# Who writes the identity halves of the scan's stacks at the border between two phases

## The chip, the core and the metric

The kernel runs on one core of a Trainium2 chip. Its engines are TensorE (PE in the profile, its weight loads PEld), VectorE (DVE), ScalarE (ACT), GpSimd (POOL) and SyncE (SP), which here only issues DMAs. The metric is device time in microseconds (us); a lower number is better.

## The reference

One inference step of one layer, for 128 context tokens and 2048 latent tokens of width 1024, in float32:

```python
def _layer(x, mod, s0, is_latent, lp):
    shift, scale, gate = jnp.split(mod, 3, axis=-1)
    h = _rmsnorm(x, lp['norm_g']) * (1.0 + scale) + shift
    proj = h @ lp['w_in']                                   # 1024 -> 4096
    r, k, v, g_a, b_gate, c_gate, u_conv, g_b = jnp.split(proj, IN_SPLITS, axis=-1)
    ...                                                     # token shift of r, k, v
    ya, s_final = _wkv(h, r, k, v, s0, lp)                  # 8 heads x 64, two directions
    ya = ya.astype(x.dtype) * jax.nn.silu(g_a)
    yb = b_gate * _short_conv(c_gate * u_conv, lp['conv_w'], is_latent) * jax.nn.silu(g_b)
    u = jnp.concatenate([ya, yb], axis=-1) @ lp['w_out']
    return x + gate * u, s_final

    # inside _wkv: the scan over tokens, for each direction and head
    def step(S, inp):
        r_t, w_t, k_t, v_t, kk_t, a_t = inp
        s_kk = jnp.einsum('bdhij,bdhj->bdhi', S, kk_t)
        S = (S * w_t[..., None, :] - s_kk[..., :, None] * (kk_t * a_t)[..., None, :]
             + v_t[..., :, None] * k_t[..., None, :])
        return S, jnp.einsum('bdhij,bdhj->bdhi', S, r_t)
```

The outputs are the normalised new context and latent tokens and the final context states of the scan.

## The kernel before

The kernel has three phases. **Phase 1** projects the tokens in six blocks with float32 products split into three matmuls (lines 182 to 184), makes the scan's operands from them and stores these in DRAM (`scr_ops`, `scr_vt` and others); its last part is the gated convolution (`groupB`, lines 546 to 621), which stores its result `ov` to `mixT` in line 621. **Phase 2** is the scan, cut into chunks of 64 tokens and 17 stages; a stage handles eight chunks of one direction (gi 0) and eight of the other (gi 1). **Phase 3** is the output projection.

A stage of phase 2 goes as follows. The operands `rr` are loaded (line 1009). Products of them are taken on TensorE (`Gm`, `Fm`, line 1019, and the transposes `Qm`, line 1028) and written out of PSUM, masked, by VectorE and ScalarE into one of three slots with the tiles `F`, `GA` and `Q` (lines 1037, 1048 and 1051). VectorE folds and transposes blocks of `GA` into `ab` (lines 1058, 1063, 1081, 1082). GpSimd inverts 32x32 triangles by substitution: 45 instructions on `ztmp` and `zt` (lines 1091 and 1094), a chain within itself. VectorE transposes the result twice (`zr`, line 1102, `zd`, line 1105), and the halves are merged into the tile `zb` by ScalarE copies and TensorE products: `zb` from `zd` (line 1111), the product `U` (line 1119) and its copy into `zd` (line 1122), the product `W` (line 1127) and its copy into `zb` (line 1130). The product `X` of `F` and `zb` (line 1171) is copied, negated, into a stack by ScalarE (line 1175). Two stacks together give the operators `E` (line 1189 and, masked, 1194), which the sequential part `S` (lines 1220 and 1246) applies chunk by chunk.

A stack is a tile of 128 partitions with two halves of columns, `b` = 0 and 1. Its bottom partitions are written new in each stage, by ScalarE (lines 1160, 1161, 1175); the top partitions of half 1 are loaded by DMA (line 956); the top partitions of half 0 hold identities and are filled once, in `presetS`. There are six stacks: `stf` (two) for line 1175 and `stg` and `sth` (two each) for lines 1160 and 1161, in even and in odd stages.

The pools decide where memory comes from. Phase 2 begins inside phase 1 with its first two stages (`early`), and at the end of phase 1 `setup_rest` opens the pools that take the memory that phase 1 gives back. There the stacks are made and filled, `zb` is cleared by GpSimd (line 907), and a third slot of `F`, `GA`, `Q` (numbers 20 and 21) is made, whose `GA21` lies over memory of phase 1's last `ov`: the first write of `GA21` waits until the store of `ov` has landed.

The engines take their instructions in order. In phase 1's recurrence and from stage 0 of the main loop on the order is written out by hand; at the border of the two phases a scheduler places instructions by its own estimate of their times.

Of the kernel before, what the change touches and what calls it, by code (L numbers as in the profile page):

```python
# [815 lines left out]
def phase2(K):  # L816
    nc, tc, A, S = K.nc, K.tc, K.A, K.S
    V, G, P, T = nc.vector, nc.gpsimd, nc.scalar, nc.tensor
    D = nc.sync.dma_start
    MF, MG, ME = (0, 1), (0, 1), (2, 3)  # L820
    B = Ctx()
# [39 lines left out]
    def setup_rest():  # L861
        O.l0 = Pool(K, "p2l0", "left")
        O.l1 = Pool(K, "p2l1", "left")
        O.pS = Pool(K, "p2S", "left", 4, PSUM)
        O.p2 = Pool(K, "p2s", "left", 2, PSUM)
        O.r2 = Pool(K, "p2r2", "right")
        new_slot(O.r2)
        cp = O.l0
        vec = cp.tile([128, 4], F32, name="vec2")
        D(vec[:], A["vec"][:, V_GW:V_GW + 4])  # L870
        B.gwh = cp.tile([128, 4], F32, name="gwh")
        V.tensor_scalar(B.gwh[:], vec[:], 0.5, None, ALU.mult)
        B.geps = cp.tile([128, 1], F32, name="geps")
        V.memset(B.geps[:], 64e-5)
        B.pc = cp.tile([64, 2, 8, 34], F32, name="pc")
        for d in range(2):
            D(B.pc[:, d], S[f"pc{d}"].rearrange("(e c) n -> c e n", c=64))

        B.fs = ring(O.l1, 2, [128, 2, 2, 8, 64], "stf", presetS)
        B.gs = ring(O.l1, 2, [128, 2, 2, 8, 64], "stg", presetS)  # L880
        B.gs2 = ring(O.r2, 2, [128, 2, 2, 8, 64], "sth", presetS)
        B.zb = O.l1.tile([128, 16, 64], F32, name="zb")
        zero(B.zb)
# [29 lines left out]

    def presetS(t_):
        for hd in range(2):
            V.tensor_copy(t_[0:64, 0, hd], B.I2[0:64].unsqueeze(1).broadcast_to((64, 8, 64)))

    def tl(shape, tag, b, pool=None, dt=F32):
        return (pool or O.l0).tile(shape, dt, tag=tag, name=f"{tag}_{K.u()}", bufs=b)
# [729 lines left out]
```

## Time and profile before

| | |
|---|---|
| median of 3 runs | 1607.61 us (1599.0 to 1609.05) |
| the profiled execution | 1596.26 us |
| its span, first to last instruction | 1594.5 us |
| PE busy | 1502.0 us (94%) |
| DVE busy | 1137.4 us (71%) |
| ACT busy | 772.3 us (48%) |
| POOL busy | 574.6 us (36%) |
| the border: from GpSimd's clearing of `zb` to its inversion of stage 3 | 948.49 to 988.83 us |

Starts and lengths are in us from the span's start. A row of a timeline has start, length, engine, line, operation, output and inputs, and the count; in square brackets stands the idle time of the engine before it and who ended it. Consecutive instructions of one engine overlap a little at their ends, so the distance from one start to the next is the time that an instruction holds its engine. A row of a table by stretches has, after the stretch, its length, the busy time and count of PE, PEld, DVE, ACT and POOL, then the granted TensorE clock, the DMA share and GB/s.

### The profile page before, as it was taken

To read this page: it belongs to the slowest core of one execution; us is meant where nothing else is said; L and a number is where in the kernel's file an instruction comes from. 1 tells how busy PE (TensorE), PEld (TensorE's weight loads), DVE (VectorE), ACT (ScalarE), POOL (GpSimd) and SP (SyncE) were. 2 spreads that over 40 slices of the span, in tenths; PEclk is the share of its full clock that TensorE was granted. 3 is DMA by queue.
4 is the path that set the end of the run, shared out by engine and by line. 5 is a ranking of instruction groups with operands and counts; after the bars stand their busy time and mean duration, and the time that the engine had idled before them with its cause. 6 is when DMAs were issued, how large, how long until landed. Compare 5 with 4: busy or idle time off the path is not lost.

```text
span 1594.5 us, 39396 instructions
## 1 busy us (share of the span) xinstructions
PE 1502.0 (94%) x16208; PEld 1382.7 (87%) x16208; DVE 1137.4 (71%) x1960; ACT 772.3 (48%) x1460; POOL 574.6 (36%) x961
## 2 busy tenths in 40 slices
PE   5899999999999999999999989999999997699998
PEld 2799999999999998999999987887888886478786
DVE  5889996673999645449984447898998986546533
ACT  4456662432555213136541127878787787323221
POOL 0033331001333100013223606888888876112221
PEclk7799999999999999999999999999999998899999
DMA  9659999663788865438886536566667655445442
GB/s 372 206 153 268 268 266 337 209 223 116 227 221 215 234 222 181 145 114 243 257 247 241 204 120 187 158 169 198 168 189 199 159 150 166 128 141 181 146 148 93
DMA packets 204580, 313.79 MB, mean 197 GB/s; under 512 B 58088, under 2 KB 147560, under 8 KB 190320
## 3 DMA queue, kind: packets, MB, share of 16 engines
q1 hardware_dynamic: 168816, 311.13, 63.1%
q10 hardware_dynamic: 35584, 0.14, 1.5%
q8 instruction: 127, 2.08, 0.6%
q14 instruction: 53, 0.43, 0.1%
HBM read 208.05 MB, written 103.17 MB: 195 GB/s over the span
## 4 chain that ended last, share of the span: by engine, by line
PE 62%; DVE 14%; POOL 9%; DMA 6%; issue 5%; ACT 2%; SPq 1%; ACTq 0%; DVEq 0%; POOLq 0%
POOL zt L1094 6%; PE psE L1189 4%; PE psu L1503 4%; PE psu L1505 4%; PE psu L1504 4%; POOL ztmp L1091 3%; PE mmb L182 2%; PE mmb L184 2%; PE mmb L183 2%; PE mmc L182 2%; PE mmc L184 2%; PE mmc L183 2%; PE psS L1220 2%; PE mmu L182 2%; PE mmu L184 2%
## 5 line engine op out<-in xcount | busy, mean ns | idle before, releaser
L1094 POOL TENSOR_TENSOR zt<-zt,ztmp 128x30 f32<-128x30 f32 (+7 forms) x510 | 218.8, 429 | 39.7
L1091 POOL TENSOR_TENSOR ztmp<-ab,zt 128x60 f32<-128x60 f32 (+7 forms) x255 | 135.6, 532 | 69.3 <-DVE ab L1082 49.7
L1220 PE MATMUL psS<-sv,E 128*64 128x64 f32 x2176 | 102.3, 229 | 25.6 <-DVE so L1246 12.5
L1220 PEld LDWEIGHTS psS<-sv,E 128*64 128x64 f32 x2176 | 81.9, 138 | 50.2 <-DVE sv L1246 17.0
L410 POOL TENSOR_TENSOR sh<-rawl 128x384 f32<-128x384 f32 (+1 forms) x48 | 47.8, 1013 | 210.2 <-ACT rawl L401 210.2
L1194 DVE TENSOR_TENSOR E<-psE,msk 128x512 f32<-128x512 f32 x136 | 90.6, 683 | 18.7 <-PE psE L1189 18.1
L1568 POOL TENSOR_TENSOR z<-z,x 128x512 f32<-128x512 f32 x32 | 42.7, 1338 | 148.5 <-DVE z L1562 98.5
L434 POOL TENSOR_TENSOR hsl<-sq,hsh 128x384 fp32r<-128x384 f32 (+1 forms) x24 | 35.7, 1488 | 140.8 <-ACT hsh L429 140.8
L1175 ACT ACTIVATE stf<-psX 64x512 f32<-64x512 f32 x136 | 80.5, 592 | 10.0 <-PE psX L1171 7.7
L1246 DVE TENSOR_TENSOR sv<-psS,pc 64x128 f32<-64x128 f32 x254 | 62.4, 272 | 20.6 <-PE psS L1220 20.1
L182 PE MATMUL mmg<-h,w 128*128 128x384 f32 (+1 forms) x216 | 70.8, 328 | 0.0
L183 PE MATMUL mmg<-h,w 128*128 128x384 f32 (+1 forms) x216 | 70.7, 327 | 0.0
L184 PE MATMUL mmg<-h,w 128*128 128x384 f32 (+1 forms) x216 | 70.6, 327 | 0.0
L219 POOL TENSOR_TENSOR hslq<-ssq,hshq 128x384 fp32r<-128x384 f32 (+1 forms) x4 | 4.8, 1206 | 174.4 <-ACT hshq L218 174.4
L182 PE MATMUL mmv<-h,w 128*128 128x384 f32 (+1 forms) x192 | 64.3, 335 | 2.6 <-ACT lf L665 2.2
L182 PE MATMUL mmb<-h,w 128*128 128x384 f32 (+1 forms) x192 | 62.8, 327 | 2.9 <-DMA w<-scr_wsp 2.9
L183 PE MATMUL mmv<-h,w 128*128 128x384 f32 (+1 forms) x192 | 63.6, 331 | 0.0
L184 PE MATMUL mmv<-h,w 128*128 128x384 f32 (+1 forms) x192 | 63.6, 331 | 0.0
L182 PE MATMUL mmc<-h,w 128*128 128x384 f32 (+1 forms) x192 | 63.1, 329 | 0.0
L184 PE MATMUL mmc<-h,w 128*128 128x384 f32 (+1 forms) x192 | 62.8, 327 | 0.2 <-DVE w L154 0.2
L184 PE MATMUL mmk<-h,w 128*128 128x384 f32 (+1 forms) x184 | 60.3, 328 | 2.7 <-DVE w L154 2.7
L184 PE MATMUL mmu<-h,w 128*128 128x384 f32 (+1 forms) x192 | 62.8, 327 | 0.0
(311 smaller groups left out, 5019.6 us busy)
## 6 DMA issues: line engine op xcount, KB each, us to landing
w<-scr_wsp SPq DMA_DIRECT2D x68, 1024.0 KB, 6.3
scr_wsp<-w SPq DMA_DIRECT2D x34, 1024.0 KB, 6.4
rr<-scr_ops SPq DMA_DIRECT2D x32, 1024.0 KB, 6.4
scr_ops<-xs SPq DMA_DIRECT2D x160, 192.0 KB, 6.7
wr<-in_win SPq DMA_DIRECT2D x34, 512.0 KB, 7.2
x<-in_x SPq DMA_DIRECT2D x17, 512.0 KB, 4.2
wadas<-in_wada SPq DMA_DIRECT2D x8, 1024.0 KB, 13.8
sv<-scr_vt SPq DMA_DIRECT2D x32, 256.0 KB, 3.8
```

Of the source, the lines that this page charges most:

```text
L182: T.matmul(ps[:, :n], w[:, 0, k], hh[:, 0, k, :n], start=k == 0, stop=False)
L183: T.matmul(ps[:, :n], w[:, 0, k], hh[:, 1, k, :n], start=False, stop=False)
L184: T.matmul(ps[:, :n], w[:, 1, k], hh[:, 0, k, :n], start=False, stop=k == 7)
L1091: G.tensor_tensor(tv, ab[:, j:j + 2, j + 2:32].unsqueeze(1).broadcast_to((128, kn, 2, n)), zt[:, :kn, j:j + 2].unsqueeze(3).broadcast_to(( ...
L1094: G.tensor_tensor(zt[:, :kn, j + 2:32], zt[:, :kn, j + 2:32], tv[:, :, r], ALU.subtract)
L1175: P.activation(g.fs[64:128, :, hd, e::2], g.ps["X"][e][hr_].rearrange("p a (b t) -> p b a t", b=2), AF.Copy, scale=-1.0)
L1189: T.matmul(pe[r, i, hd, :].rearrange("p (b t) -> p b t", b=2), lt[:, b, hd, us.start + k + i], rt[:, :, hd, us.start + k + i], start=True, ...
L1194: V.tensor_tensor(g.E[n][:, k:k + 2].rearrange("p a b c -> p (a b) c"), pe[:].rearrange("p a b c -> p (a b) c"), B.msk[:, ME[g.d]].unsquee ...
L1220: T.matmul(g.sp[i // 4][r, q, hd, :], g.E[n][:, k, hd, r], g.sv[:, u, hd, :], start=True, stop=True)
L1503: T.matmul(ps[:], mh[:, n], hi[:, cs], start=start and n == 0, stop=False)
L1504: T.matmul(ps[:], mh[:, n], lo[:, cs], start=False, stop=False)
L1505: T.matmul(ps[:], ml[:, n], hi[:, cs], start=False, stop=stop and n == 3)
```

## The change

`presetS`, called once for each of the six stacks in `setup_rest`, has two copies of 64 partitions x 512 columns from the identity tile `I2`. They are issued on GpSimd (`G`) instead of VectorE (`V`):

```diff
     def presetS(t_):
         for hd in range(2):
-            V.tensor_copy(t_[0:64, 0, hd], B.I2[0:64].unsqueeze(1).broadcast_to((64, 8, 64)))
+            G.tensor_copy(t_[0:64, 0, hd], B.I2[0:64].unsqueeze(1).broadcast_to((64, 8, 64)))
```

Twelve instructions change their engine, and the scheduler arranges what lies around them anew. On GpSimd, this is the place between the inversion of stage 1 (`zt_1023`) and that of stage 2 (`zt_1081`):

```order
 L1091 TENSOR_TENSOR ztmp_1024_8995<-ab_1022_8987,zt_1023_8989 128x60
 L1094 TENSOR_TENSOR zt_1023_8989<-zt_1023_8989,ztmp_1024_8995 128x15x2 x2
+L916 COPY stf0_9576<-I2_8357 64x512 x2
+L916 COPY stf1_9577<-I2_8357 64x512 x2
+L916 COPY stg0_9582<-I2_8357 64x512 x2
+L916 COPY stg1_9583<-I2_8357 64x512 x2
 L907 MEMSET zb_9594 128x1024
+L916 COPY sth0_9588<-I2_8357 64x512 x2
+L916 COPY sth1_9589<-I2_8357 64x512 x2
 L1091 TENSOR_TENSOR ztmp_1107_10009<-ab_1077_9742,zt_1081_9774 128x60
 L1094 TENSOR_TENSOR zt_1081_9774<-zt_1081_9774,ztmp_1107_10009 128x30 x2
```

Eight copies now stand ahead of the clearing of `zb`, and four between it and the inversion of stage 2.

On VectorE, the same place after the last masked product of phase 1, before the change:

```order
L874 MEMSET geps_9571 128x1
L916 COPY stf0_9576<-I2_8357 64x512 x2
L916 COPY stf1_9577<-I2_8357 64x512 x2
L916 COPY stg0_9582<-I2_8357 64x512 x2
L619 TENSOR_TENSOR ov3_5_9533<-ov3_5_9533,bsv3_5_9529 128x320
L916 COPY stg1_9583<-I2_8357 64x512 x2
L1102 STREAM_TRANSPOSE zr_1066_9603<-zt_989_8598 128x32x16
L872 TENSOR_SCALAR gwh_9569<-vec2_9567 128x4
L1105 STREAM_TRANSPOSE zd_1067_9605<-zr_1066_9603 128x512
L916 COPY sth0_9588<-I2_8357 64x512 x2
L916 COPY sth1_9589<-I2_8357 64x512 x2
L1037 TENSOR_TENSOR GA20_9562<-psGm0_2_1069_9642,mkg_8350 128x512
```

and with it:

```order
L874 MEMSET geps_9571 128x1
L1102 STREAM_TRANSPOSE zr_1066_9603<-zt_989_8598 128x32x16
L619 TENSOR_TENSOR ov3_5_9533<-ov3_5_9533,bsv3_5_9529 128x320
L1105 STREAM_TRANSPOSE zd_1067_9605<-zr_1066_9603 128x512
L872 TENSOR_SCALAR gwh_9569<-vec2_9567 128x4
L1037 TENSOR_TENSOR GA21_9565<-psGm1_2_1073_9679,mkg_8350 128x512
L1037 TENSOR_TENSOR GA21_9565<-psGm1_2_1074_9680,mkg_8350 128x512
L1102 STREAM_TRANSPOSE zr_1089_9849<-zt_1023_8989 128x32x16
L1058 SCALAR_TENSOR_TENSOR dg_1071_9664<-GA21_9565,hm_8361 128x256
L1037 TENSOR_TENSOR GA20_9562<-psGm0_2_1069_9642,mkg_8350 128x512
L1037 TENSOR_TENSOR GA20_9562<-psGm0_2_1070_9643,mkg_8350 128x512
L1058 SCALAR_TENSOR_TENSOR dg_1071_9664<-GA20_9562,hm_8361 128x256
```

The transposes `zr` and `zd` of stage 0 follow at once, and `GA21` is now written ahead of `GA20`. On TensorE the product `U` of stage 0, which reads `zr`, moves in between the products `Gm` of stage 2.

On ScalarE, from the copies of `zd` into `zb` to the copies of `W`, before:

```order
L1111 COPY zb_9594<-zd_1067_9605 32x16x32 x4
L1160 COPY sth1_9589<-GA11_8375 64x8x64
L1161 COPY sth1_9589<-Q11_8376 64x8x64
L1160 COPY sth0_9588<-GA10_8372 64x8x64
L1161 COPY sth0_9588<-Q10_8373 64x8x64
L1122 COPY zd_1067_9605<-psU_0_1068_9609 32x512 x2
L1051 COPY F20_9561<-psFm0_2_1078_9744 128x4x64
L1051 COPY F20_9561<-psFm0_2_1079_9745 128x4x64
L1075 ACTIVATE zt_1081_9774<-ab_1077_9742,ph_8363 128x16
L1048 COPY Q21_9566<-psQm1_2_1076_9733 128x4x2x64
L1048 COPY Q20_9563<-psQm0_2_1080_9765 128x4x2x64
L1130 ACTIVATE zb_9594<-psW_0_1075_9700 32x16x32 x2
```

and with the change, where the four copies to `sth` stand ahead of this piece:

```order
L1048 COPY Q21_9566<-psQm1_2_1076_9733 128x4x2x64
L1048 COPY Q20_9563<-psQm0_2_1080_9765 128x4x2x64
L1051 COPY F20_9561<-psFm0_2_1078_9744 128x4x64
L1051 COPY F20_9561<-psFm0_2_1079_9745 128x4x64
L1075 ACTIVATE zt_1081_9774<-ab_1077_9742,ph_8363 128x16
L1051 COPY F21_9564<-psFm1_2_1082_9780 128x4x64
L1051 COPY F21_9564<-psFm1_2_1083_9781 128x4x64
L1111 COPY zb_9594<-zd_1067_9605 32x16x32 x4
L1122 COPY zd_1067_9605<-psU_0_1068_9609 32x512 x2
L1130 ACTIVATE zb_9594<-psW_0_1075_9700 32x16x32 x2
```

The three steps of the merge (lines 1111, 1122, 1130) now follow each other with nothing in between, after the copies of `Q` and `F` of stage 2. On SyncE the store of `ov` (line 621) moves ahead of the two loads of `stg` (line 956).

## The prediction

> **What bounds the kernel now.** I read the page's busy times first, then the waits of GpSimd, then the border of the two phases engine by engine.
>
> ```profile
> span 1594.5 us, 39396 instructions
> PE 1502.0 (94%) x16208; PEld 1382.7 (87%) x16208; DVE 1137.4 (71%) x1960; ACT 772.3 (48%) x1460; POOL 574.6 (36%) x961
> ```
>
> Over the whole span TensorE is busy 94% of the time, but the change lies in one short place, so the place must be read alone. GpSimd's waits between 960 and 1340 us, and the first instructions after its waits:
>
> ```profile
> POOL ztmp L1091 <- DVE ab L1082: 21.0, 3, 14.5
> 948.49 0.95 POOL L907 MEMSET zb<- 128x1024 f32 x1 [40.76 <-PE mmb L184]
> 963.94 0.29 POOL L1091 TENSOR_TENSOR ztmp<-ab,zt 128x60 f32<-128x60 f32 x1 [14.50 <-DVE ab L1082]
> 988.83 0.29 POOL L1091 TENSOR_TENSOR ztmp<-ab,zt 128x60 f32<-128x60 f32 x1 [2.51 <-DVE ab L1082]
> ```
>
> GpSimd waits three times: 14.50 us for stage 2, 2.51 us for stage 3, and 21.0 - 17.0 = 4.0 us near the end. In between it inverts without a pause. So the start of stage 3's inversion, 988.83, sets the pace of the whole scan: a microsecond there is a microsecond at the end, later or earlier. What sets that start is the work at the border, in this stretch:
>
> ```profile
> 948.50:972.00 23.50, 17.23 (x442) 14.24 (x440) 17.43 (x35) 21.55 (x41) 7.67 (x19) 0.84 0.86 223
> ```
>
> Here TensorE is busy only 17.23 of 23.5 us, VectorE 17.43, and **ScalarE 21.55**. Its rows:
>
> ```profile
> 952.33 0.61 ACT L1161 COPY stg<-Q 64x512 f32<-64x512 f32 x1
> 953.45 0.63 ACT L1073 ACTIVATE zt<-idt 128x512 f32<-128x512 f32 x1 [0.51 <-DVE gwh L872]
> 954.11 0.22 ACT L1074 COPY zt<-ph 128x16 f32<-128x16 f32 x1
> 954.25 2.52 ACT L1111 COPY zb<-zd 32x512 f32<-32x512 f32 x4
> 956.79 0.62 ACT L1160 COPY sth<-GA 64x512 f32<-64x512 f32 x1
> 959.10 1.18 ACT L1122 COPY zd<-psU 32x512 f32<-32x512 f32 x2
> 960.30 0.65 ACT L1051 COPY F<-psFm 128x256 f32<-128x256 f32 x2
> 961.59 0.42 ACT L1075 ACTIVATE zt<-ab,ph 128x16 f32<-128x16 f32 x1 [0.64 <-DVE ab L1063]
> 961.90 1.05 ACT L1048 COPY Q<-psQm 128x512 f32<-128x512 f32 x2
> 962.85 1.20 ACT L1130 ACTIVATE zb<-psW 32x512 f32<-32x512 f32 x2
> 965.05 3.65 ACT L1175 ACTIVATE stf<-psX 64x512 f32<-64x512 f32 x6 [0.33 <-PE psX L1171]
> ```
>
> It waits 0.51 + 0.64 + 0.33 = 1.48 us in all, and ends with the copies of `X` into the stacks, without which TensorE can't build `E`, nor go on to the products that lead to stage 3's `ab`. VectorE's rows at the same place:
>
> ```profile
> 948.80 0.91 DVE L916 COPY stf<-I 64x512 f32<-64x512 f32 x1
> 951.31 0.48 DVE L619 TENSOR_TENSOR ov<-ov,bsv 128x320 f32<-128x320 f32 x1
> 951.71 0.75 DVE L916 COPY stg<-I 64x512 f32<-64x512 f32 x2
> 952.38 1.03 DVE L1102 STREAM_TRANSPOSE zr<-zt 128x512 f32<-128x512 f32 x1
> 953.45 0.71 DVE L1105 STREAM_TRANSPOSE zd<-zr 128x512 f32<-128x512 f32 x1
> 954.08 1.38 DVE L916 COPY sth<-I 64x512 f32<-64x512 f32 x4
> 955.39 2.46 DVE L1037 TENSOR_TENSOR GA<-psGm,mkg 128x512 f32<-128x512 f32 x4
> 959.49 2.06 DVE L1063 STREAM_TRANSPOSE ab<-dg 128x1024 f32<-128x1024 f32 x1
> ```
>
> **What VectorE loses.** The copies hold it from 948.80 to 951.31, 951.71 to 952.38 and 954.08 to 955.39: 2.51 + 0.67 + 1.31 = 4.49 us. Without them the rest up to `GA` (`ov` 0.40 by its distance to the next start, `zr` to the end of `zd` 1.70) runs from 948.85 to 950.95. But `GA21` now comes first, and it must wait until the store of `ov` has landed. `ov` ends at about 948.85 + 1.03 + 0.48 = 950.3. The landing times, of this store alone and of the four such stores from 900 us on:
>
> ```profile
> DMA to landing us min/median/max: 1.8/1.8/1.8
> DMA to landing us min/median/max: 1.8/4.1/6.3
> ```
>
> I take 1.8, since it is the same store, and no load of `stg` is ahead of it now: `GA` starts at 952.1. Bounds are 950.95 (nothing to wait for) and 950.3 + 6.3 = 956.6. Of the 4.49 us **3.3** are left (955.39 to 952.1); 1.2 become a new wait. Behind it on VectorE stand the same instructions as before up to `ab`, 4.10 us later by the rows, so the transpose of line 1063 ends at 952.1 + 4.10 + 2.06 = 958.3 instead of 961.55.
>
> **What ScalarE does with it.** By the distances of its rows: the `stg` copies end at 952.94; line 1073 no longer waits, 0.65, to 953.6; the four `sth` copies 2.31 (956.79 to 959.10), to 955.9; line 1074 0.14, to 956.05; two `Q` 0.95, to 957.0; two `F` 0.65, to 957.65. Then line 1075 waits for `ab` until 958.35, a wait of 0.7, and takes 0.31; two `F` 0.65, to 959.3; four `zb` (line 1111) 2.54, to 961.85; two `zd` (line 1122) 1.20, to 963.05. Here is what the new order costs. Before, `F` and `Q` stood between line 1122 and line 1130, and covered the product `W`. Now nothing does. TensorE's rows for `U`, `W` and `X`:
>
> ```profile
> 953.56 1.49 PE L1119 MATMUL psU<-zr,GA 32*32 32x32 f32 x64 [3.23 <-DVE gwh L872]
> 960.92 1.19 PE L1127 MATMUL psW<-zb,zd 32*32 32x32 f32 x61
> 963.73 0.28 PE L1171 MATMUL psX<-F,zb 64*64 64x128 f32 x2
> 963.84 2.54 PE L1171 MATMUL psX<-F,zb 64*64 64x128 f32 x62
> ```
>
> `W` can end 1.2 after 963.05, line 1130 starts at 964.35 and its first half ends at 964.95; 0.3 later (962.85 + 0.6 to 963.73 before) `X` starts, whose first quarter takes 0.64 of 2.54, and the first copy of line 1175 starts at about **966.0 instead of 965.05**. From there on ScalarE's order is that of before. The product `U` of stage 1, which stood behind the first `E` on TensorE, now lies in the shadow of `W`; that shortens nothing that ScalarE waits for. **Sum: +1.0 us**, the saved 3.3 us notwithstanding.
>
> **What GpSimd takes on.** No copy of this size is in the trace. Next to it:
>
> ```profile
> 964.30 0.57 POOL L1094 TENSOR_TENSOR zt<-zt,ztmp 128x30 f32<-128x30 f32 x2
> L1215 POOL MEMSET sv<- 64x128 f32 x8 | 1.3, 198 | 0.0
> L1213 POOL COPY sv<-held 64x128 f32<-64x128 f32 x2 | 0.6, 286 | 0.0
> L1568 POOL TENSOR_TENSOR z<-z,x 128x512 f32<-128x512 f32 x32 | 42.7, 1338 | 148.5 <-DVE z L1562 98.5
> ```
>
> A clearing takes 0.198 us for 128 columns and 0.95 for 1024 (line 907): 0.84 ns a column and 0.09 us fixed. If the copy's extra 88 ns are fixed too, a copy of 512 columns takes 0.61 us; if all of its 286 ns grow with size, 1.14; if the fixed part is 0.09, 0.88, which I take. A two-operand instruction of this size, 1.34, is the upper end. With 0.07 between instructions (963.94 + 0.29 to 964.30) eight copies take 7.6 us from 948.49 on, the clearing of `zb` ends at 957.1, and ScalarE needs it at 959.3: hidden. The last four copies end at about 961, and stage 2's inversion, whose `ab` comes 3.3 us earlier (960.6), can start near there instead of 963.94; it has 2.51 us of slack on top. So GpSimd adds nothing.
>
> The Trainium skill, GPSIMD Engine Reference, section 4.1, puts a one-input operation at about line rate; worked out from the clearing's 0.84 ns a column that would be an estimate of 0.5 us, and the sum would stay +1.0.
>
> VectorE can hold GpSimd up, though:
>
> ```profile
> 1010.28 1.32 POOL L1091 TENSOR_TENSOR ztmp<-ab,zt 128x60 f32<-128x60 f32 x1
> 1010.30 1.12 DVE L1081 TENSOR_TENSOR dg<-ab 128x512 f32<-128x512 f32 x1
> ```
>
> The same 128x60 instruction took 0.29 at 963.94; beside line 1081 it took 1.0 longer, the length of VectorE's instruction. Up to the clearing, line 619 (0.48) and one of like size, a fold of `GA`, stand there: I allow 0.9, and the clearing ends at 958.0, still hidden. The Trainium skill, GPSIMD Engine Reference, section 1 (Specifications), says that VectorE's instructions with two SBUF inputs contend with GpSimd for their common way to the SBUF. These two rows agree, and the 0.9 is what they make of that rule here.
>
> **The sum.** The profiled execution took 1596.26, 1.76 more than its span; with +1.0 it would take 1597.3. The median of the runs lies 11.35 above it, and the runs themselves are 10 us apart, which is more than anything here. Carried to the median: **1608.6 us**. About 1%, 16 us, is what a measurement of this kernel can tell from no change.
>
> **Rivals.**
>
> *The saving reaches the end.* For it: the transposes' delay is the largest gap of TensorE here (3.23 us before `U`), and it goes. Against it: ScalarE's work is the same, and only its waits, 1.48 us, could go. Price: -1.5 at most, 1606.1. Chance 0.14.
>
> *The clearing of `zb` comes too late.* The place is GpSimd's queue: line 1111 waits for it, and `W`, `X`, `E` behind that. It decides where 948.49 + 8 copies + 1.0 + 0.9 passes 959.3, with copies over 1.11 us each, gap included. With 1.41 (the two-operand row) it is 8 x 0.30 = 2.4 more: +3.4, 1611.0. Slower by 1% would take copies of about 3 us. Chance 0.14.
>
> *The store lands late.* With 4.1 instead of 1.8 line 1075 waits 2.3 more: +3.3, 1610.9; with 6.3, +5.5. It is the median of the window, but the slow ones were behind weight loads. Chance 0.10.
>
> *TensorE slows down in the new hole.* The clock before:
>
> ```profile
> 950.00:953.50 3.50, 0.33 (x13) 0.09 (x4) 3.47 (x11) 2.98 (x7) 0.00 (x0) 1.00 0.71 190
> 954.00:961.00 7.00, 5.93 (x95) 5.13 (x91) 6.97 (x13) 6.76 (x14) 0.00 (x0) 0.52 0.92 215
> ```
>
> After about 3 idle us (busy 0.33 of 3.5) the granted clock was 0.52 for 7 us. Now TensorE does `Fm` by about 958.2 and then has nothing until the first `zd` of line 1122 at 962.6: 4.4 us. If the half clock falls on `W` and the first of `X`, their 1.2 + 0.6 up to double: +1.8 on top, 1610.4. Against it: the old low stretch had U and `Fm` in it too, and parts of `W` ran at it. Chance 0.12. The Trainium skill, TensorE: Matmul & The Clock Gate, Part 1, says the clock halves after an idle window of some 3.4 us and comes back after as long a busy one; by it this rival is what happens, and the row agrees on the half clock, but shows it for twice as long.
>
> That nothing moves at all is ruled out by the instruction order: twelve instructions change queue.
>
> **How the numbers follow.** My forecast, +1.0 (own range 0 to +2, 1607.6 to 1609.6), has the remaining 0.50. The cases reach from -1.5 to +5.5. The scatter of executions is added: the lowest of the three runs less 1.5 is 1597.5, the highest, 1609.05, plus 3.4 is 1612.5; together they are the range. No case comes near 16 us, so faster and slower by over 1% have only the scatter's tails: 0.03 and 0.04, which leaves 0.93 for the same.
>
> **What would show it.** VectorE: `zr` at about 949, then a wait of about 1 us ahead of `GA`, ended by the store's landing. GpSimd: twelve copies of about 0.9 us, `zb` cleared by 957 to 958. ScalarE: a wait of more than 1 us ahead of line 1130, ended by `W`, and line 1175 first at about 966. GpSimd's inversion of stage 3 about 1 us later after the last matmul of phase 1 than the 40.3 us of before. I am wrong if the copies take over 1.1 us each, if line 1130 doesn't wait, or if stage 3's inversion starts earlier.

## The result, and the profile after

The changed kernel took 1605.03 us (median of 12 runs, 1598.32 to 1614.04), the kernel before 1600.66 us on the same chip (12 runs, 1593.35 to 1609.05). The ratio is **1.0036, with a 95% interval from 1.0019 to 1.0053**: 4.4 us by the medians, 3 to 8.5 us by the interval. It is slower, by less than 1%. The profiled execution took 1604.56 us:

```profile
PE 1507.2 (94%) x16208; PEld 1388.5 (87%) x16208; DVE 1137.2 (71%) x1948; ACT 770.7 (48%) x1460; POOL 574.9 (36%) x973
```

This line of the page, the busy times of the engines, is nearly that of before; twelve instructions have changed sides. GpSimd's timeline at the border:

```profile
949.58 2.53 POOL L916 COPY stf<-I 64x512 f32<-64x512 f32 x4 [40.76 <-PE mmb L184]
954.29 0.95 POOL L907 MEMSET zb<- 128x1024 f32 x1
955.18 2.52 POOL L916 COPY sth<-I 64x512 f32<-64x512 f32 x4
962.45 0.28 POOL L1091 TENSOR_TENSOR ztmp<-ab,zt 128x60 f32<-128x60 f32 x1 [4.74 <-DVE ab L1082]
994.17 0.29 POOL L1091 TENSOR_TENSOR ztmp<-ab,zt 128x60 f32<-128x60 f32 x1 [9.48 <-DVE ab L1082]
```

GpSimd is done with its new work 4.74 us before it is needed, so the copies are hidden. But its wait ahead of stage 3 has grown from 2.51 to 9.48 us (2.6 us of these 7 only because it begins stage 2 that much earlier). Phase 1 itself ended 1.1 us later in this execution (949.58, before 948.49), so from here on times are counted from that end, and the **border** is the time from it to the start of stage 3's inversion: 988.83 - 948.49 = 40.34 us before, 994.17 - 949.58 = **44.59 us** after. The 4.25 us more are near the 4.4 us of the medians. The timelines of VectorE and of ScalarE in the same place:

```profile
950.86 0.78 DVE L619 TENSOR_TENSOR ov<-ov,bsv 128x320 f32<-128x320 f32 x1
952.20 1.06 DVE L872 TENSOR_SCALAR gwh<-vec 128x4 f32<-128x4 f32 x1
953.56 1.29 DVE L1037 TENSOR_TENSOR GA<-psGm,mkg 128x512 f32<-128x512 f32 x2 [0.31 <-DMA scr_mixT<-ov]
958.01 2.05 DVE L1063 STREAM_TRANSPOSE ab<-dg 128x1024 f32<-128x1024 f32 x1
```

```profile
960.10 0.42 ACT L1075 ACTIVATE zt<-ab,ph 128x16 f32<-128x16 f32 x1 [1.22 <-DVE ab L1063]
960.93 2.51 ACT L1111 COPY zb<-zd 32x512 f32<-32x512 f32 x4
963.47 1.18 ACT L1122 COPY zd<-psU 32x512 f32<-32x512 f32 x2
967.24 1.20 ACT L1130 ACTIVATE zb<-psW 32x512 f32<-32x512 f32 x2 [2.60 <-PE psW L1127]
969.90 1.19 ACT L1175 ACTIVATE stf<-psX 64x512 f32<-64x512 f32 x2 [1.46 <-PE psX L1171]
972.09 1.20 ACT L1175 ACTIVATE stf<-psX 64x512 f32<-64x512 f32 x2 [1.00 <-PE psX L1171]
```

VectorE is ahead: `GA` starts 3.98 us after the end of phase 1, before 6.90. ScalarE doesn't profit: it now waits 2.60 us for `W` and 1.46 and 1.00 us for `X`, where before it waited 0.33 us once. The first copy of line 1175 stands at 20.32 us, before at 16.56. TensorE's timeline, and the stretches ahead of and behind its hole, in which the third number from the right is the granted clock:

```profile
956.76 2.69 PE L1019 MATMUL psFm<-rr 64*64 64x128 f32 x64 [1.20 <-DVE GA L1037]
964.18 0.23 PE L1127 MATMUL psW<-zb,zd 32*32 32x32 f32 x1 [4.73 <-ACT zd L1122]
967.88 5.87 PE L1171 MATMUL psX<-F,zb 64*64 64x128 f32 x64 [0.43 <-ACT zb L1130]
```

```profile
953.00:959.00 6.00, 3.64 (x74) 3.08 (x70) 5.62 (x9) 5.75 (x12) 4.70 (x8) 1.00 0.97 196
963.00:975.00 12.00, 10.39 (x204) 9.91 (x206) 0.71 (x1) 6.52 (x12) 10.16 (x24) 0.50 0.99 257
```

TensorE stands still for 4.73 us ahead of `W`; then the granted clock is 0.50 for 12 us, and `X` takes 5.87 us instead of 2.54.

The half clock is only a part of these 5.87 us. In the run `sth` only (below) `X` ran at half clock too, and took 3.64 us. One microsecond out of `X` in each, the changed kernel first, with `X`'s instructions alone (PE, PEld and ACT):

```profile
968.50:969.50 1.00, 1.00 (x14) 1.00 (x12) 0.00 (x0) 0.50 1.22 167
966.00:967.00 1.00, 1.00 (x24) 1.00 (x23) 0.00 (x0) 0.50 1.07 231
```

At the same clock the rows have 14 matmuls against 24: in the trace they start two at a time, 0.21 us apart, in the changed kernel, and four at a time there. So `X` is slower also by the order of its own products on TensorE.

### The profile page after: what moved, and what is told of

Read it like the earlier page. It is cut to its first block, busy times and chain, and to the rows that moved or that the text cites. A ratio compares the mean times of both kernels' runs of the same rounds, so it can differ in the third digit from the quotient of the medians.

```text
span 1602.8 us, 39402 instructions
## 1 busy us (share of the span) xinstructions
PE 1507.2 (94%) x16208; PEld 1388.5 (87%) x16208; DVE 1137.2 (71%) x1948; ACT 770.7 (48%) x1460; POOL 574.9 (36%) x973
## 4 chain that ended last, share of the span: by engine, by line
PE 61%; DVE 20%; DMA 9%; issue 5%; ACT 2%; POOL 1%; SPq 1%; ACTq 0%; DVEq 0%; POOLq 0%
PE psE L1189 5%; PE psu L1503 4%; PE psu L1505 3%; PE psu L1504 3%; PE psS L1220 2%; PE mmb L182 2%; PE mmb L184 2%; PE mmb L183 2%; PE mmc L182 2%; PE mmc L184 2%; PE mmc L183 2%; DVE ab L1063 2%; PE psGm L1019 2%; PE mmu L184 2%; PE mmu L182 2%
## 5 line engine op out<-in xcount | busy, mean ns | idle before, releaser
L1175 ACT ACTIVATE stf<-psX 64x512 f32<-64x512 f32 x136 | 80.3, 591 | 13.3 <-PE psX L1171 11.1
L434 POOL TENSOR_TENSOR hsl<-sq,hsh 128x384 fp32r<-128x384 f32 (+1 forms) x24 | 32.2, 1342 | 141.8 <-ACT hsh L429 141.8
L184 PE MATMUL mmu<-h,w 128*128 128x384 f32 (+1 forms) x192 | 62.9, 328 | 0.0
L182 PE MATMUL mmu<-h,w 128*128 128x384 f32 (+1 forms) x192 | 62.9, 328 | 0.0
```

The source lines that it names most:

```text
L182: T.matmul(ps[:, :n], w[:, 0, k], hh[:, 0, k, :n], start=k == 0, stop=False)
L184: T.matmul(ps[:, :n], w[:, 1, k], hh[:, 0, k, :n], start=False, stop=k == 7)
L1175: P.activation(g.fs[64:128, :, hd, e::2], g.ps["X"][e][hr_].rearrange("p a (b t) -> p b a t", b=2), AF.Copy, scale=-1.0)
```

## The experiments

The main reading of each is the border and the steps in it, in us after the end of phase 1. A row's start, less the start of GpSimd's first instruction after its wait for `mmb`, gives each number; the last column is the ratio to the kernel before with its 95% interval.

| kernel | copies on | order at the border | W | L1130 | first L1175 | border | ratio |
|---|---|---|---|---|---|---|---|
| before | VectorE | before | 12.34 | 14.36 | 16.56 | 40.34 | |
| before, again | VectorE | before | 12.14 | 14.42 | 16.62 | 40.59 | 1.0000 (0.9973 to 1.0027) |
| changed | GpSimd | changed | 14.60 | 17.66 | 20.32 | 44.59 | 1.0036 (1.0019 to 1.0053) |
| changed, again | GpSimd | changed | 15.35 | 18.40 | 21.06 | 48.96 | 1.0054 (1.0033 to 1.0074) |
| order only | VectorE | changed | 18.26 | 21.32 | 23.97 | 47.48 | 1.0082 (1.0055 to 1.0109) |
| held, mended | GpSimd | before (ScalarE) | 10.79 | 13.85 | 17.46 | 39.42 | 1.0009 (0.9983 to 1.0035) |
| held, two engines | GpSimd | before (ScalarE, TensorE) | 10.78 | 13.24 | 16.86 | 40.56 | 1.0012 (0.9987 to 1.0036) |
| sth only | 4 on GpSimd | before | 13.29 | 15.70 | 19.32 | 41.01 | 1.0008 (0.9986 to 1.0031) |
| zb first | GpSimd | a third one | 13.40 | 15.36 | 19.30 | 42.79 | 1.0028 (1.0005 to 1.0051) |
| zb late | VectorE | L1111 later | 16.50 | 18.56 | 22.01 | 43.77 | 1.0031 (1.0011 to 1.0051) |
| 18 products | GpSimd | changed | 15.42 | 17.33 | 19.52 | 47.14 | 1.0047 (1.0025 to 1.0069) |
| 104 products | GpSimd | changed, W before U | 33.96 | 35.21 | 37.15 | 60.17 | 1.0131 (1.0101 to 1.0162) |

**zb first.** The clearing of `zb` moves ahead of the copies on GpSimd:

```diff
+        B.zb = O.l1.tile([128, 16, 64], F32, name="zb")
+        zero(B.zb)
         B.fs = ring(O.l1, 2, [128, 2, 2, 8, 64], "stf", presetS)
         ...
-        B.zb = O.l1.tile([128, 16, 64], F32, name="zb")
-        zero(B.zb)
```

> This is the changed kernel with one move: GpSimd clears zb before it fills the identities, not between stg and sth. All twelve copies stay on GpSimd. ScalarE's order becomes L1111, sth, L1074, Q21, Q20, L1122, F20, L1075, F21, L1130, so that W has F20 and F21 to cover it. The main reading is the length of the border, from the end of GpSimd's last wait for phase 1 (L184) to the start of stage 3's inversion: 40.34 us before, 44.59 us after. Theory 1 (the new order leaves W uncovered, TensorE stands still for 4.7 us ahead of it and then runs W, X and E at half clock): the hole ahead of W is under 2 us, L1130 waits less than 1 us, X takes about 2.6 us and not 5.87, the border is 38.5 to 41 us and the time within 0.3% of before, perhaps 1 us under it. Theory 2 (the copies on GpSimd cost the time themselves, by its port or by GpSimd being late): the border stays at 43 to 45 us and the ratio at 1.003 to 1.004. Theory 3 (what is lost is VectorE's wait for the store of ov): VectorE is as far ahead as after, so 43 to 45 us as well.

Measured: a border of 42.79 us, between the two. Its timeline on TensorE and ScalarE, and the stretch around it:

```profile
950.41 1.97 PE L1028 MATMUL psQm<-idt,rr 128*128 128x128 f32 x8 [0.96 <-DVE GA L1037]
956.47 2.89 PE L1019 MATMUL psFm<-rr 64*64 64x128 f32 x32 [0.54 <-ACT Q L1048]
961.01 1.73 PE L1119 MATMUL psU<-zr,GA 32*32 32x32 f32 x56
961.25 1.20 ACT L1130 ACTIVATE zb<-psW 32x512 f32<-32x512 f32 x2 [1.47 <-PE psW L1127]
965.19 2.42 ACT L1175 ACTIVATE stf<-psX 64x512 f32<-64x512 f32 x4 [2.73 <-PE psX L1171]
```

```profile
950.50:970.50 20.00, 18.19 (x286) 15.93 (x288) 10.06 (x15) 14.86 (x29) 12.28 (x28) 0.50 1.08 241
```

ScalarE hands over `zd` early here, but on TensorE all of `Fm` still stands ahead of `W`, and stage 1's `U` (1.73 us) ahead of `X`. The order on ScalarE was mended, and the waits moved to TensorE: to its order, and to its clock, which was at half for 20 us, over `Fm`, `W` and `X`. No hole led to that; the clock fell at the end of a pause of 0.96 us, TensorE's longest up to there. Theory 1 missed here, since line 1130 waited 1.47 us and `X` took 5.5: its first form, which spoke of ScalarE and the hole, was too narrow. What TensorE's order and what its clock cost here the run doesn't tell apart.

**zb late.** The kernel before, with `zb` cleared six times:

```diff
-        zero(B.zb)
+        [zero(B.zb) for _ in range(6)]
```

> This is the kernel before, with zb cleared six times in a row, so that it is ready about 4.7 us later, near the time at which it is in the changed kernel (955.2 us); the copies of the identities stay on VectorE. On the other engines only one thing moves: L1111 stands behind the four sth copies on ScalarE and no longer ahead of them. Theory 1 (the order of ScalarE around W and the half clock): W keeps its cover here (F20, L1075 and Q21 stand between L1122 and L1130), so the border is 40.0 to 41 us against 40.34 us before, and the time is the same as before. Theory 2 (zb ready late is itself the price): the border is 43 to 45 us.

Measured: 43.77 us, as theory 2 had it, but for another reason. GpSimd's clearings and VectorE's copies lay side by side in the timeline:

```profile
950.92 5.62 POOL L907 MEMSET zb<- 128x1024 f32 x5 [40.76 <-PE mmb L184]
952.08 3.58 DVE L916 COPY stf<-I 64x512 f32<-64x512 f32 x3
961.98 2.47 DVE L1037 TENSOR_TENSOR GA<-psGm,mkg 128x512 f32<-128x512 f32 x4
994.69 0.29 POOL L1091 TENSOR_TENSOR ztmp<-ab,zt 128x60 f32<-128x60 f32 x1
```

Three copies took 3.58 us instead of 1.07, and `GA` came at 11.06 us instead of 6.90. The last row has no wait in brackets: GpSimd was inverting stage 2 until then, which it had begun 4.1 us later than before (19.59 us, before 15.45). This run delayed VectorE, not `zb` alone, and tells nothing between the theories.

**The hole filled.** `W` of stage 0 is issued behind `Fm1` in the program and products that nobody reads stand between them, 104 and then 18 (the lines that make them, with 18; those that place them are left out):

```diff
+    def warm(s):
+        f0, n = stage(s).g[0].F, 18
+        wm = O.pS.tile([128, 4, 128], F32, tag="S", name="warm")
+        for i in range(n):
+            T.matmul(wm[0:64, i % 4, :], f0[0:64, i % 4, 0:64], B.idt[0:64, :], start=True, stop=True)
```

> This is the changed kernel with 104 matmuls of 64x128 that nobody reads, put on TensorE between Fm1 and W, where it stands still for 4.73 us in the changed kernel; the order of the other engines is the changed kernel's. At the 41 ns that one takes at full clock they fill about 4.3 us of the 4.73. W then stands ahead of all of U. Theory 1a (of the 4.25 us that the border grew, about 3 are half clock on W, X and E): the granted clock is 1.00 from 964 to 976 us, X takes 2.5 to 3 us and not 5.87, the border is 41 to 42.5 us, the ratio 1.000 to 1.002. Theory 1b (W uncovered costs by ScalarE's order alone and the clock is only a bystander): X is shorter, but the border stays at 44 to 45 us. Theory 2 (the copies on GpSimd): 44 to 45 us.

Measured: each product is two matmuls in the trace, of 108 ns and not 41, so they overran the hole by far and delayed `W` to 33.96 us. Its timeline, TensorE's rows and then ScalarE's, and the stretch behind `W`:

```profile
960.57 22.54 PE L1390 MATMUL warm<-idt,F 64*64 64x128 f32 x205
983.03 1.11 PE L1127 MATMUL psW<-zb,zd 32*32 32x32 f32 x58
984.28 1.20 ACT L1130 ACTIVATE zb<-psW 32x512 f32<-32x512 f32 x2 [19.46 <-PE psW L1127]
```

```profile
983.00:989.00 6.00, 6.00 (x205) 5.75 (x206) 0.71 (x1) 3.71 (x7) 0.83 (x3) 1.00 0.02 3
```

Its time is no answer, but behind the products the clock was 1.00, and that gives the chain at full clock: from `W` to the first copy of `X` 37.15 - 33.96 = 3.19 us, where the changed kernel took 20.32 - 14.60 = 5.72 (there with most of stage 1's `U` within `W` as well).

> The changed kernel with nothing moved and 18 products of 64x128 (36 matmuls in the trace) that nobody reads put between Fm1 and W. In the run with 104 of them one of the 208 matmuls took 108 ns, so these take 3.9 us and end about when W can start (963.9 against 964.2 us). Theory 1a (half clock on W, U, X and E is most of the loss): with the clock at 1.00 from W on, W's start to the first copy of X (L1175) takes 3.2 us, as it did in that run, and not 5.7; the border is 40.5 to 42 us, the ratio 1.000 to 1.002. Theory 1b (ScalarE's order alone): the border is 44 to 45 us whatever the clock.

Measured: `W` at 15.42 us with the clock at 1.00, line 1130 1.91 us later (3.06 in the changed kernel), the first line 1175 at 19.52. From `W` to there it took 4.10 us, 1.6 less than in the changed kernel, but not the 3.2 expected: here too most of stage 1's `U` lies within `W`, and the clock fell to 0.50 again at 965.9, in the first quarter of `X`. Its timeline on ScalarE and TensorE, and the stretch of `W`:

```profile
964.79 1.20 ACT L1130 ACTIVATE zb<-psW 32x512 f32<-32x512 f32 x2 [1.45 <-PE psW L1127]
965.42 2.35 PE L1171 MATMUL psX<-F,zb 64*64 64x128 f32 x22 [0.52 <-ACT zb L1130]
970.77 3.69 PE L1171 MATMUL psX<-F,zb 64*64 64x128 f32 x42 [3.00 <-issue]
972.80 2.51 ACT L1175 ACTIVATE stf<-psX 64x512 f32<-64x512 f32 x4 [4.63 <-PE psX L1171]
```

```profile
962.80:965.80 3.00, 2.44 (x135) 2.32 (x136) 0.71 (x1) 1.53 (x3) 2.53 (x7) 1.00 1.08 333
```

In the middle of `X` TensorE stands still for 3.00 us and waits for nothing that the profile shows; the rest of `X` ran at half clock. The border, 47.14 us, and the ratio, 1.0047, are therefore no gain. What the half clock costs is shown for parts of the leg up to the first line 1175, not for the whole time.

**sth only.** Four of the twelve copies move, and the order of ScalarE stays (the diff is against the changed kernel, so `eng=V` takes the other eight back to VectorE):

```diff
-        B.gs2 = ring(O.r2, 2, [128, 2, 2, 8, 64], "sth", presetS)
+        B.gs2 = ring(O.r2, 2, [128, 2, 2, 8, 64], "sth", lambda t_: presetS(t_, G))
         ...
+    def presetS(t_, eng=V):
```

> Only the four copies into sth go to GpSimd, the eight into stf and stg stay on VectorE. zb is cleared as early as before, and the order of ScalarE is that of before, L1111 ahead of sth. VectorE loses 4 of 12 copies, 1.3 to 1.5 us. Theory 1 (order and clock): the border is 39.3 to 40.5 us against 40.34 us before, the time the same as before or up to 1 us less. Theory 2 (each copy on GpSimd costs the border its share, by contention or lateness): a third of the 4.25 us, so 41.5 to 42 us.

Measured: 41.01 us, half a microsecond over what theory 1 asked and half under theory 2; the time is that of before. VectorE gained nothing: three `stf` copies took 2.31 us beside GpSimd's, instead of 1.07. Before, and here:

```profile
949.64 1.07 DVE L916 COPY stf<-I 64x512 f32<-64x512 f32 x3
949.56 2.31 DVE L916 COPY stf<-I 64x512 f32<-64x512 f32 x3
```

ScalarE so waited 2.17 us for VectorE, where before it waited 0.51, and the first line 1175 came 2.76 us later than before; behind it 2.09 of these were made up.

**Order only, and held: the two that decide.** The words of the border are moved in the program and ScalarE's order is then held to it (of the diffs the moves alone are shown). With the copies on VectorE and the changed kernel's order:

```diff
+        move("gh10@0 gh11@0 gh00@0 zi_@2", "Gm0@2")
+        move("gh01@1", "gsL0@1")
+        move("Qm0@2 Qe1@2 Qe0@2", "Qm1@2")
+        move("c0@0 c1@0 bu@0 W@0 n@0 X0@0", "Fe1@2")
+        held = tc.manual_schedule(engines={mybir.EngineType.Activation})
```

> The counterpart: the copies stay on VectorE and zb is cleared early, as in the kernel before, but ScalarE's order at the border is that of the changed kernel (sth, Q21, Q20, F20, L1075, F21, and then L1111, L1122, L1130 in a row); TensorE's order follows and is nearly the changed kernel's, with all of stage 1's U ahead of X. Theory 1: the border grows although no copy has moved, from 40.34 to 43.5 to 47 us, since VectorE's 3.3 us of lateness are added to the changed order; the time is 3 to 7 us above before. Theory 2 (copies on GpSimd): no change, 40 to 41 us.

Measured, in its timeline (lines below 1071 have moved by three in this kernel and the held ones, so that line 1133 is 1130 of before, and 1178 is 1175):

```profile
948.85 0.95 POOL L907 MEMSET zb<- 128x1024 f32 x1 [40.75 <-PE mmb L184]
967.11 0.23 PE L1130 MATMUL psW<-zb,zd 32*32 32x32 f32 x1 [3.57 <-ACT zd L1125]
970.17 1.20 ACT L1133 ACTIVATE zb<-psW 32x512 f32<-32x512 f32 x2 [2.60 <-PE psW L1130]
972.82 1.19 ACT L1178 ACTIVATE stf<-psX 64x512 f32<-64x512 f32 x2 [1.46 <-PE psX L1174]
996.33 0.29 POOL L1094 TENSOR_TENSOR ztmp<-ab,zt 128x60 f32<-128x60 f32 x1 [9.49 <-DVE ab L1085]
```

Not one copy has moved, and the border grows to 47.48 us, with the waits of the changed kernel: 2.60 ahead of the copies of `W`, 1.46 ahead of those of `X`, and 9.49 (there 9.48) on GpSimd. ScalarE also waits 3.47 us for `Qm` here, which stands on TensorE behind products that wait 1.36 us for VectorE's late `GA`; so the 7.1 us are the price of this order with VectorE late and not the changed kernel's own. The time grew more, by 0.0055 to 0.0109 of 1600 us or 9 to 17 us, than these 7.1 us of one execution.

The other way round, with the copies on GpSimd and the order of before:

```diff
+        move("gh10@0 gh11@0 gh00@0 zi_@2 c0@0", "Gm0@2")
+        move("gh01@1 bu@0", "gsL0@1")
+        move("W@0 Qe1@2 Qe0@2 n@0", "pre@2")
+        move("Fm1@2 L1@3 Fa1@2 Fe1@2 X0@0", "n@0")
+        held = tc.manual_schedule(engines={mybir.EngineType.Activation})
```

> The copies are on GpSimd as in the changed kernel, eight ahead of the clearing of zb, but ScalarE's order at the border is written out by hand so that it is that of the kernel before: L1073, L1074, L1111, sth, L1122, F20, L1075, Q21, Q20, L1130, F21. Only one pair of sth copies stands otherwise, ahead of L1074. TensorE then has Qm and Fm ahead of W, and half of stage 1's U ahead of X. VectorE has none of the twelve copies. Border before 40.34 us, changed kernel 44.59. Theory 1 (the changed order is the price): the border is 38.5 to 40.5 us and the time 0 to 2 us under before (ratio 0.998 to 1.001). Theory 2 (the copies on GpSimd cost by themselves, by making zb late or by slowing VectorE): 43 to 45 us, ratio 1.003 or more.

In this first form the word `L1@3`, the load of stage 3's operands, was left ahead of `Fm1@2`, which so read those operands and waited 9.59 us for them; `W` at 10.80 and line 1130 at 13.86 were the only use of the run (border 48.74 us, ratio 1.0052). Mended, as the diff above shows it:

> All twelve copies on GpSimd as in the changed kernel, ScalarE's order that of the kernel before (as in the run held, but with the load of stage 3's operands behind the last product of stage 2 that reads the tile, so that Fm1 doesn't wait for it). In the run held W started 10.80 us after the end of phase 1 (14.60 in the changed kernel, 12.34 before) and L1130 at 13.86 (17.66, 14.36), ahead of a wait of 9.59 us for that load. Without this wait, theory 1 (the order is the price) gives the first L1175 at 15.5 to 17 us, a border of 38.5 to 40.5 us and a time within 2 us of before (ratio 0.998 to 1.001). Theory 2 (the copies on GpSimd) gives 43 to 45 us and a ratio of 1.003 or more.

Measured, in the timeline and in the stretch around `W`:

```profile
947.41 2.53 POOL L916 COPY stf<-I 64x512 f32<-64x512 f32 x4 [40.78 <-PE mmb L184]
961.26 1.20 ACT L1133 ACTIVATE zb<-psW 32x512 f32<-32x512 f32 x2 [0.65 <-PE psW L1130]
964.87 3.64 ACT L1178 ACTIVATE stf<-psX 64x512 f32<-64x512 f32 x6 [1.06 <-PE psX L1174]
986.83 0.28 POOL L1094 TENSOR_TENSOR ztmp<-ab,zt 128x60 f32<-128x60 f32 x1 [3.93 <-DVE ab L1085]
```

```profile
955.50:964.00 8.50, 7.80 (x196) 7.36 (x196) 6.01 (x9) 6.80 (x15) 2.83 (x10) 0.50 1.07 240
```

All twelve copies are on GpSimd, and the border is 39.42 us, within what theory 1 asked; the time is that of before. The first line 1175, at 17.46 us, lies just past the 15.5 to 17 that it asked. The stretch shows more: the clock was at half over `W` here too, and `W` to line 1130 took the same 3.06 us as in the changed kernel. With two `F`, line 1075 and two `Q` in between, ScalarE waited 0.65 us for it instead of 2.60. Then also with TensorE's order:

> As the run before it, with TensorE's order written out as well: Gm, U of stage 0, Fm0, Qm, W, Fm1, X, E and only then U of stage 1, as in the kernel before; GA20 comes ahead of GA21 again, so that VectorE doesn't wait for the store of ov at once. Theory 1: the border is 38 to 40 us, the ratio 0.997 to 1.000. If U of stage 1 ahead of X was the larger part, this run is 1 us or more under the one before it; if ScalarE's order was, they are equal. Theory 2: 43 to 45 us.

```profile
994.45 0.29 POOL L1094 TENSOR_TENSOR ztmp<-ab,zt 128x60 f32<-128x60 f32 x1 [5.04 <-DVE ab L1085]
```

Measured: 40.56 us (994.45 - 953.89), just over what theory 1 asked, and the same time as the run before it within the intervals. So that `U` stands partly ahead of `X` isn't the larger part; what both runs have and the changed kernel has not is `Fm1` behind `W`, and ScalarE's work between lines 1122 and 1130.

ScalarE's waits, from the end of phase 1 to the first line 1175, show the same. They sum to 1.48 us before, 1.77 in held two, 2.42 in held mended and 5.28 in the changed kernel (1.22 + 2.60 + 1.46); line 1175 stands at 16.56, 16.86, 17.46 and 20.32. Its work is the same in all four, and the line comes later by what ScalarE waits more. By the times alone the two held runs (up to 1.0035 and 1.0036) and the changed kernel (from 1.0019) are not clearly apart; the waits and the border are what tells them apart.

The border is not line 1175 plus a constant, though. From there to stage 3 it took 23.78 and 23.97 us in the kernel before and 23.70 in held two, but 21.96 in held mended and 21.69 in sth only. The first three have a pause of TensorE of 1.10 to 1.57 us within stage 1's `U`, which ends with nothing that the profile shows, and a stretch at half clock behind it; the other two have neither. In the kernel before:

```profile
970.04 0.56 PE L1119 MATMUL psU<-zr,GA 32*32 32x32 f32 x23 [1.32 <-issue]
971.50:974.50 3.00, 3.00 (x38) 2.71 (x32) 2.12 (x5) 2.92 (x6) 2.61 (x6) 0.50 0.03 12
```

So the 0.92 us by which held mended lies under the kernel before were won behind line 1175, and not ahead of it, where it is 0.90 us late.

**The scatter of the border.**

> The changed kernel once more, to see how far its border moves from one execution to another with the place at which the granted clock falls and rises. Theory 1: if the clock is at half over W, U, X and E again, the border is 44 to 45 us; if it is full there, 40.5 to 42 us. Theory 2: 44 to 45 us in either case.

Measured, in the timeline and in the stretch from `W` on:

```profile
972.00 1.20 ACT L1130 ACTIVATE zb<-psW 32x512 f32<-32x512 f32 x2 [2.59 <-PE psW L1127]
1002.56 0.29 POOL L1091 TENSOR_TENSOR ztmp<-ab,zt 128x60 f32<-128x60 f32 x1 [13.73 <-DVE ab L1082]
```

```profile
969.00:988.00 19.00, 18.57 (x274) 16.43 (x276) 3.68 (x7) 12.20 (x21) 16.18 (x37) 0.50 0.52 138
```

The border is 48.96 us. Up to the first line 1175 the steps are those of the first profile (5.71 us from `W`), but the clock stayed at half for 19 us, on through `E` and the first products of the scan, though TensorE was busy 18.57 of them; that cost 3.6 us more from there to stage 3 (27.90 us, in the first profile 24.27).

> The kernel before once more, for the scatter of its border. Its first profile had 40.34 us with the clock at half for 9.5 us of it; the changed kernel's two profiles had 44.59 and 48.96. Theory 1: 40 to 42 us, since ScalarE's F and Q copies cover W at either clock. If it lies at 44 us or above, the single profiles don't separate the kernels and only the times do.

Measured: 40.59 us, 0.25 from the first profile. The kernel before keeps its border, the changed one has a longer and a more variable one. The runs' times don't tell whether the clock makes the scatter: over the changed kernel's first 12 runs the time goes with the mean granted clock (1614.04 us at 0.967, 1598.32 at 0.982, correlation -0.78), but over the six of its second profile it doesn't (0.32), and over two sets of 29 runs of the kernel before the correlation is -0.28 and 0.11.

## Why the prediction was right, and where it was short

**The direction and the mechanism held.** I forecast a loss from ScalarE's new order in spite of the saving on VectorE, and the deciding runs show that: the order alone costs, and the copies with the order of before cost nothing that was measured. The signs are there: line 1130 waits more than 1 us for `W`, `GA` waits for the store of `ov`, and `zb` is clear in time. That the time lies in the range of 1597.5 to 1612.5 us says little: the range is 15 us wide for the scatter (its top counts +3.4, not the +5.5 of my largest case), and the kernel before, at 1600.66, lies in it too. My 1608.6 us started from a median of three runs, 1607.61, that twelve runs put 7 us lower; this hid that the step itself was too small.

**The size was short: +1.0 us, own range 0 to +2; measured 3 to 8.5 by the times, 4.25 in the profile.** By its steps, from the end of phase 1:

- *VectorE keeps 3.3 of 4.49 us.* Near: `ab` (line 1063) ends 2.6 us earlier than before (10.48 instead of 13.06). The wait for the store of `ov` was 0.31 us and not 1.15, but line 619 took 0.78 instead of 0.48 and line 872 took 1.06 instead of 0.13 beside GpSimd's copies. This slowing fell on VectorE; I had only allowed for one on GpSimd.
- *GpSimd adds nothing.* Right. Eight copies took 4.71 us to the start of the clearing (949.58 to 954.29), 0.59 each, under my 0.88 plus gap and near the lower bound; `zb` was clear at 5.66 us and wanted at 11.35.
- *ScalarE up to line 1122:* I had its end at 14.56, it was 15.07.
- *The step that failed: "`W` can end 1.2 after 963.05", and `X`'s first quarter after it.* From the end of line 1122 to line 1130 I had 1.3 us; it took 2.59. From there to the first line 1175 I had 1.65; it took 2.66. With the 0.51 from above these are the 2.81 us by which line 1175 came after my 17.51. For `W` I took a row with TensorE's order of before. In the new order stage 1's `U` lies within `W`, which I put in its shadow: 1.25 us from `W` to line 1130 without it (104 products), 1.91 with it (18 products), so 0.66; and the half clock makes 3.06 of the 1.91, so 1.15. That is 1.81 for a miss of 1.29, since I had allowed 0.52 too much: I counted all of `W` from the end of line 1122, and it starts 0.47 us ahead of that. For `X`, some 0.7 of the 1.01 are the half clock (2.66 against 1.94 in the run with 104 products, where the clock was 1.00), and 0.3 are my own working: the row of before has 2.20 between the two starts, and I had shortened it to 1.65.
- *"From there on ScalarE's order is that of before."* Its order is, but not its pace: with `X` at 5.87 us, by the half clock and by the order of its products two at a time, it waits another 1.00, and in the second profile the half clock lasted into the scan. From the first line 1175 to stage 3 it took 24.27 and 27.90 us, before 23.78 and 23.97.

**The rivals.** The clearing of `zb` too late: false, and the copies were far from the 1.11 us from which it decides. The store late: false, 0.31 us. The saving at the end: false in the changed kernel, and even with the order of before (the two held runs) it bought nothing that the times can tell. **TensorE at half clock over `W` and `X` is what happened**, on top of the forecast, and in the changed kernel the clock fell inside the new hole. That the hole brought it on is not shown: with `zb` first there was no such hole and the clock was at half for 20 us, and it was at half over `W` in the held runs too. The rival's price of +1.8 was about right for what I counted (1.15 + 0.7), though it left out the rest of `X` and `E`; its chance, 0.12, was too small. What I held against it, that the old low stretch had also touched `W`, missed the point: a slow `W` behind cover costs 0.65 us of waiting, and without it 2.60. The Trainium skill, TensorE: Matmul & The Clock Gate, Part 1, said by its rule of an idle window of about 3.4 us that the clock would halve. The 4.73-us hole agrees with that, the pause of 0.96 us with `zb` first doesn't; nor does its one busy window of 3.4 us for the way back agree, since TensorE stayed at 0.50 for 12 us with 10.39 busy, and for 19 with 18.57.

**What stays open.** How much of the 4.25 us the half clock makes in all was not isolated, since the run with 18 products met a pause of 3.00 us of unknown origin; nor was it tried how much is the order of `X`'s products. Why the clock falls without a hole, and why it stays low for 12 us in one execution and 19 in another, was not tried. No version beat the kernel before; the held ones equal it.

## What to carry to other kernels

When a scheduler places instructions by its own estimates, moving an operation to an idle engine can change the order on all the others, as it did here; price the new order at its uncovered steps, and not the operation. A chain that hands work between two engines in turn (copy, product, copy, product) needs other work between its links on both: here the same slow `W`, 3.06 us to line 1130, cost 0.65 us of waiting with cover and 2.60 without. The clock was at half somewhere on the border in every run, with a hole and without; price such a chain at half clock until a row shows otherwise.

## What the hardware showed that I had not expected

- Copies with one input on VectorE are slowed by GpSimd as two-input instructions are: 64x512 copies took 0.36 us each in the kernel before (1.07 for three), 0.77 beside GpSimd's copies (2.31) and 1.19 beside its clearings (3.58). The Trainium skill, GPSIMD Engine Reference, section 1 (Specifications), names, beside VectorE's instructions with two SBUF inputs, those in a two-port performance mode; the slowing agrees, and that these copies run in this mode no run here shows.
- Even a 128x4 instruction (line 872) took 1.06 us instead of 0.13 while GpSimd copied.
- The granted clock stayed at 0.50 for 12 to 20 us with TensorE busy most of the time (10.39 of 12, 18.57 of 19, 18.19 of 20 us), and it also fell there in a pause of only 0.96 us.
